# Last sums and residual of one feed-forward taken in token halves, and residual tiles loaded ahead of the norm

## Chip, cores and metric

The kernel runs on one core of a Trainium2 chip. The metric is the device time of one execution in microseconds, lower is better; the time before is the median of three executions.

## The reference, cut to what matters

Two layers over 1024 tokens of width 1024, all in float32. Each sub-layer stands between two RMS norms and adds its normed result to the residual stream `h`:

```python
def rms_norm(x, g, eps=1e-6):
    xf = x.astype(jnp.float32)
    y = xf * lax.rsqrt(jnp.mean(xf * xf, axis=-1, keepdims=True) + eps)
    return (y * g.astype(jnp.float32)).astype(x.dtype)
...
def swiglu(y, wg, wu, wd):
    return (jax.nn.silu(y @ wg) * (y @ wu)) @ wd
...
    for l in range(DEPTH):
        y = rms_norm(h, norm_g[l, 0])
        ...
        h = h + rms_norm(y, norm_g[l, 1])
        y = swiglu(rms_norm(h, norm_g[l, 2]), w_gate[l], w_up[l], w_down[l])
        h = h + rms_norm(y, norm_g[l, 3])
```

What stands at the second "..." is the mixer: gated DeltaNet and top-k sparse attention in layer 0, stick-breaking attention and a gated linear recurrence in layer 1, then an output projection of the two concatenated results.

## The kernel before, in words

**Tiling.** Features lie on the 128 partitions and tokens in the columns. The 1024 tokens are taken in two halves of 512, so an activation of width 1024 is eight tiles of 128x512. Every large product is done in three passes: each operand is split into a rounded high part and a low part (the rest), and high x high, low x high and high x low are summed in PSUM (`passes`, L239). ACT makes the high part and DVE or POOL the low part (`split`, L192 and L196). Weights come in units of 128x1024 (`wload`, L227): two loads of 256 KB into `wraw`, split into `whi` and `wlo`; four buffers of each hold two units.

**Stages.** For each half: `outproj` (L418) sums the output projection from the split mixer results `cat`; `after_out` (L528) norms it and adds the residual; `ffn` (L449) does the SwiGLU in six groups of hidden tiles; `after_ffn` (L533) norms and adds again. `h` lives in DRAM between them. `residual` (L385) is the common body: `inv_rms` (L309) sums the squares over partitions with a matmul on ones (L313) and takes the inverse root on ACT (L315, L316). Then for each of the eight tiles the residual is loaded into a `hld` tile (three buffers, L396), the sum is multiplied by gain and inverse root (L397), the residual is added (L398) and the result stored (L399). Where `late` is set, `y_tile` (L334) at once splits the result, still unnormed, into `yhi` (ACT, L339) and `ylo` (DVE, L343) for the next product, and `norms` sums its squares (L302, L305, L306).

**The last group of an FFN.** The eight sums of the last group are added to `part` (L489), each followed by its square and the squares' add. The very last FFN of the kernel uses `down_halves` (L497) in their place: for the first 256 columns all eight sums, then for the other 256, each half with squares of its own (L509), and `last_residual` (L513) norms and adds half by half (L524, L525). In `down_halves` a weight unit is loaded anew for each half.

**The pool `act`** (L416) holds 16 tiles of 128x512. It is shared: `outproj` keeps its 16 split `cat` tiles there (L428), an FFN the eight split hidden tiles of a group of four (L469).

**What sets the order.** A scheduler puts the instructions in order on each engine, by priorities and the program's order; `first()` (L185) raises a block's priority. `pace` lets pieces of the sparse attention run between weight units in FFN(0, half 0). In `run` (L1288), FFN(0, half 1) is followed by `after_ffn` whose generator is started, and `outproj(1, 0)` is woven in with it (L1342 to L1348).

Of the kernel before, what the change touches and what calls it, by code (L numbers as in the profile page):

```python
# [12 lines left out]
F32 = mybir.dt.float32  # L13
F32R = mybir.dt.float32r
BF = mybir.dt.bfloat16
U32 = mybir.dt.uint32
AF = mybir.ActivationFunctionType
OP = mybir.AluOpType
# [4 lines left out]
P = 128  # L23
S = 1024
D = 1024
HS = 512
NT = 4
KD = 8
# [83 lines left out]
class Trunk:  # L112
# [272 lines left out]
    def residual(self, l, i, src, dst, parts, acc, nxt, box, late=False):  # L385

        nc = self.nc
        with self.first():
            r = self.inv_rms(acc, "rs", "b")
            acc = None  # L390
            y = Y()
            for k in range(KD):
                p = parts[k]
                rows = slice(k * P, (k + 1) * P)
                h = self.t(self.hp, [P, HS], "hld", bufs=3)
                nc.sync.dma_start(h, src[rows])  # L396
                nc.vector.scalar_tensor_tensor(p, p, self.ng(l, i, k), r, op0=OP.mult, op1=OP.mult)  # L397
                nc.vector.tensor_tensor(out=p, in0=p, in1=h, op=OP.add)  # L398
                nc.sync.dma_start(dst[rows], p)  # L399
                if late:  # L400
                    self.y_tile(y, k, p, self.ng(*nxt, k))
                elif nxt is not None:
                    acc = self.sumsq(acc, k, p)
            if late:
                self.norms(y, parts, nxt[1] == 0)
                box.append(y)
        if nxt is not None and not late:
            yield
            with self.first():
                r = self.inv_rms(acc, "rs", "b")  # L410
            yield
            with self.first():
                box.append(self.to_y(*nxt, parts, r))
        yield
# [98 lines left out]
    def last_residual(self, src, dst, parts, halves):  # L513
        nc = self.nc
        with self.first():
            hs = []
            for k in range(KD):
                hs.append(self.t(self.tail, [P, HS], "tail"))
                nc.sync.dma_start(hs[k], src[k * P:(k + 1) * P])
            for i, (c, acc) in enumerate(halves):  # L520
                r = self.inv_rms(acc, ("rs", "rd")[i], "b")
                for k in range(KD):
                    p, h = parts[k][:, c], hs[k][:, c]
                    nc.vector.scalar_tensor_tensor(p, p, self.ng(1, 3, k), r, op0=OP.mult, op1=OP.mult)  # L524
                    nc.vector.tensor_tensor(out=p, in0=p, in1=h, op=OP.add)  # L525
                    nc.sync.dma_start(dst[k * P:(k + 1) * P, c], p)

    def after_out(self, l, half, parts, box, late=False):  # L528
        cols = slice(half * HS, (half + 1) * HS)
        src = self.ins["x"][:, cols] if l == 0 else self.h[1][half]  # L530
        return self.residual(l, 1, src, self.h[2 * l][half], *parts, (l, 2), box, late)
# [756 lines left out]
    def run(self):  # L1288
        tc = self.tc
        every = lambda gen: deque(gen, maxlen=0)  # L1290
# [5 lines left out]
        y = self.first_norm(0)  # L1296
# [3 lines left out]
        y = self.first_norm(1)  # L1300
        with self.since(mark - BOOST0):
            self.deltanet_setup(pool)
            self.dsa_setup(pool)
            b = self.dsa(pool, 0)
# [9 lines left out]
        y1, o, f, y = y, [], [], []  # L1314
# [3 lines left out]
        self.tm_store(U_VB, y1, self.vb[1])  # L1318
        self.slow = slow
        every(self.after_out(0, 0, o, y, True))  # L1320
        every(self.ffn(0, y[0], f))
        every(self.after_ffn(0, 0, f, y, True))
        self.proj_d(0, y[1])
        self.finish()
        m0.close()
# [7 lines left out]
        y0, o, f, y = y[1], [], [], []  # L1333
        every(self.outproj(0, 1, o, "hld"))
        r = self.after_out(0, 1, o, y)
# [6 lines left out]
        r = self.after_ffn(0, 1, f, y, True)  # L1342
        next(r)
        o0, y0 = [], []
        g = self.outproj(1, 0, o0, "stage")
# [3 lines left out]
        r = self.after_out(1, 0, o0, y0)  # L1349
# [8 lines left out]
        f0, o, f, y = [], [], [], []  # L1358
        g = self.ffn(1, y0[0], f0)
# [7 lines left out]
        r = self.after_out(1, 1, o, y)  # L1367
# [105 lines left out]
```

## Time and profile before

| | us |
|---|---|
| median of three executions (2882.89 to 2889.29) | 2888.78 |
| the profiled execution's own time | 2889.96 |
| its span, first to last instruction | 2888.2 |
| PE (TensorE) busy | 2819.6 (98%) |
| DVE (VectorE) busy | 1674.9 (58%) |
| ACT (ScalarE) busy | 1580.7 (55%) |
| POOL (GpSimd) busy | 1117.3 (39%) |
| mean granted TensorE clock | 0.992 |

The span is one execution recorded by the hardware; the time around it is 1.8 us. A busy share is an average over the whole span, so a stage is read from windows and timelines of its own. In a timeline row, what stands in brackets is how long the engine was idle before it and what ended the wait. The granted clock is 1.00 at 2.4 GHz and 0.50 at 1.2 GHz; a mean between them is a stretch with both.

### The profile page before, as it was taken

To read this page: it belongs to the slowest core of one execution; us is meant where nothing else is said; L and a number is where in the kernel's file an instruction comes from. 1 tells how busy PE (TensorE), PEld (TensorE's weight loads), DVE (VectorE), ACT (ScalarE), POOL (GpSimd) and SP (SyncE) were. 2 spreads that over 40 slices of the span, in tenths; PEclk is the share of its full clock that TensorE was granted. 3 is DMA by queue.
4 is the path that set the end of the run, shared out by engine and by line. 5 is a ranking of instruction groups with operands and counts; after the bars stand their busy time and mean duration, and the time that the engine had idled before them with its cause. 6 is when DMAs were issued, how large, how long until landed. Compare 5 with 4: busy or idle time off the path is not lost. (4 is left out here: it accounts for less than half of the span.)

```text
span 2888.2 us, 42444 instructions
## 1 busy us (share of the span) xinstructions
PE 2819.6 (98%) x14850; PEld 2352.7 (81%) x14850; DVE 1674.9 (58%) x3037; ACT 1580.7 (55%) x2893; POOL 1117.3 (39%) x916
## 2 busy tenths in 40 slices
PE   8999999999999998999999999999999999999997
PEld 6888898878887876988888888889778778888886
DVE  8757964674756557377655235836665545822235
ACT  5555854667666575264665334536666554543334
POOL 3424332344435342255554323226555532333322
PEclk9999999999999999999999999999999999999999
DMA  6443456344333334445333333644333223543333
GB/s 208 135 125 105 149 164 196 97 138 120 98 120 102 104 120 137 146 151 184 114 112 99 95 95 121 238 159 129 95 99 103 92 86 118 185 144 95 97 97 106
DMA packets 261748, 366.69 MB, mean 127 GB/s; under 512 B 23296, under 2 KB 111392, under 8 KB 261536
## 3 DMA queue, kind: packets, MB, share of 16 engines
q1 hardware_dynamic: 261536, 364.00, 40.0%
q8 instruction: 117, 1.92, 0.3%
q14 instruction: 95, 0.78, 0.1%
HBM read 306.23 MB, written 57.67 MB: 126 GB/s over the span
## 5 line engine op out<-in xcount | busy, mean ns | idle before, releaser
L196 POOL TENSOR_TENSOR wlo<-wraw,whi 128x512 fp32r<-128x512 f32 x422 | 588.8, 1395 | 1292.0 <-PE acc L252 526.7
L192 ACT ACTIVATE whi<-wraw 128x512 fp32r<-128x512 f32 x844 | 522.3, 625 | 480.5 <-PE acc L252 385.2
L196 DVE TENSOR_TENSOR wlo<-wraw,whi 128x512 fp32r<-128x512 f32 x422 | 346.2, 821 | 426.5 <-PE acc L252 334.7
L252 PE MATMUL acc<-yhi,whi 128*128 128x512 f32 x2064 | 582.6, 398 | 8.1 <-ACT whi L192 5.9
L252 PE MATMUL acc<-ylo,whi 128*128 128x512 f32 x2064 | 583.4, 398 | 1.0 <-DVE ylo L343 0.9
L252 PE MATMUL acc<-yhi,wlo 128*128 128x512 f32 x2064 | 537.5, 396 | 0.0
L252 PE MATMUL acc<-act,whi 128*128 128x512 f32 (+1 forms) x1984 | 508.1, 393 | 7.0 <-DVE part L489 1.8
L252 PEld LDWEIGHTS acc<-yhi,whi 128*128 128x128 f32 x2064 | 385.3, 189 | 92.7 <-ACT whi L192 6.4
L252 PEld LDWEIGHTS acc<-ylo,whi 128*128 128x128 f32 x2064 | 387.1, 189 | 88.0 <-issue 6.2
L252 PEld LDWEIGHTS acc<-yhi,wlo 128*128 128x128 f32 x2064 | 383.7, 188 | 86.2 <-issue 9.0
L252 PEld LDWEIGHTS acc<-act,whi 128*128 128x128 f32 x1984 | 365.3, 190 | 95.1 <-issue 7.9
L252 PE MATMUL acc<-act,wlo 128*128 128x512 f32 (+1 forms) x992 | 267.1, 387 | 0.8 <-POOL wlo L196 0.8
L252 PEld LDWEIGHTS acc<-act,wlo 128*128 128x128 f32 x992 | 182.4, 188 | 38.1 <-POOL wlo L196 1.6
L959 ACT ACTIVATE pen<-sc,tk 128x384 bf16<-128x384 f32 (+4 forms) x155 | 155.3, 1002 | 41.8 <-DVE tk L963 38.2
L489 DVE TENSOR_TENSOR part<-acc,part 128x512 f32<-128x512 f32 x152 | 103.5, 685 | 66.7 <-PE acc L252 66.6
L192 ACT ACTIVATE act<-stage 128x512 fp32r<-128x512 f32 x104 | 65.3, 629 | 132.9 <-DVE stage L468 114.1
L196 POOL TENSOR_TENSOR act<-stage,act 128x512 fp32r<-128x512 f32 x88 | 117.6, 1337 | 33.7 <-ACT act L192 30.7
L461 DVE TENSOR_TENSOR stage<-acc,stage 128x512 f32<-128x512 f32 x66 | 45.5, 690 | 109.4 <-ACT stage L219 107.3
L306 DVE TENSOR_TENSOR ssq<-ssq,sq 128x512 f32<-128x512 f32 (+1 forms) x119 | 97.2, 817 | 18.7 <-ACT sq L305 15.8
L960 DVE TENSOR_SCALAR tk<-tk 128x1 uint32<-128x1 f32 x186 | 39.2, 211 | 110.6 <-ACT pen L959 109.8
L252 PE MATMUL acc<-whi,yhi 128*128 128x256 f32 x640 | 98.8, 287 | 1.4 <-DVE stage L561 1.0
L252 PE MATMUL acc<-whi,ylo 128*128 128x256 f32 x640 | 97.2, 285 | 0.0
(461 smaller groups left out, 4009.7 us busy)
## 6 DMA issues: line engine op xcount, KB each, us to landing
wraw<-in_w_units_dram SPq DMA_DIRECT2D x844, 256.0 KB, 2.7
h<-part SPq DMA_DIRECT2D x40, 256.0 KB, 4.0
hld<-h SPq DMA_DIRECT2D x40, 256.0 KB, 4.8
qkvT<-stage SPq DMA_DIRECT2D x24, 256.0 KB, 2.3
kT<-kbT SPq DMA_DIRECT2D x24, 256.0 KB, 3.9
vv<-vb SPq DMA_DIRECT2D x24, 256.0 KB, 2.9
qkv<-qkvT SPq DMA_DIRECT2D x18, 256.0 KB, 3.1
part<-in_x_dram SPq DMA_DIRECT2D x16, 256.0 KB, 5.1
```

The costliest lines, as they stand in the source:

```text
L192: nc.scalar.activation(hi, src, AF.Copy)
L196: e.tensor_tensor(out=lo[:, c], in0=src[:, c], in1=hi[:, c].bitcast(F32), op=OP.subtract)
L252: mm(ps, l, r, start=first and g not in begun, stop=last and end[g] == i)
L306: nc.vector.tensor_tensor(out=acc, in0=acc, in1=sq, op=OP.add)
L461: nc.vector.tensor_tensor(out=s, in0=pg, in1=s, op=OP.mult)
L489: nc.vector.tensor_tensor(out=parts[d], in0=ps, in1=parts[d], op=OP.add)
L959: sc.activation(pen, s, AF.Sign, scale=sg, bias=nb, accum_out=n)
L960: v.tensor_scalar(rej.bitcast(U32), n, th, float(1 << b), op0=OP.is_lt, op1=OP.mult)
```

## The change

In every `residual`, the eight residual tiles are loaded into tiles of the pool `act` ahead of `inv_rms`, in place of `hld` tiles loaded one by one behind it. FFN(0, half 0) takes its last sums by `down_halves`, and a new `residual_halves` norms, adds and splits first 256 columns of all eight tiles, then the other 256; it stores whole tiles in the second round. Lines behind the first edit move: L397 and L398 become L399 and L400 in `residual`, and in `residual_halves` the product is L545, the add L546, the low part L548.

```diff
--- before.py
+++ after.py
@@ -386,14 +386,16 @@
 
         nc = self.nc
         with self.first():
+            hs = []
+            for k in range(KD):
+                hs.append(self.act())
+                nc.sync.dma_start(hs[k], src[k * P:(k + 1) * P])
             r = self.inv_rms(acc, "rs", "b")
             acc = None
             y = Y()
-            for k in range(KD):
+            for k, h in enumerate(hs):
                 p = parts[k]
                 rows = slice(k * P, (k + 1) * P)
-                h = self.t(self.hp, [P, HS], "hld", bufs=3)
-                nc.sync.dma_start(h, src[rows])
                 nc.vector.scalar_tensor_tensor(p, p, self.ng(l, i, k), r, op0=OP.mult, op1=OP.mult)
                 nc.vector.tensor_tensor(out=p, in0=p, in1=h, op=OP.add)
                 nc.sync.dma_start(dst[rows], p)
@@ -524,6 +526,30 @@
                     nc.vector.scalar_tensor_tensor(p, p, self.ng(1, 3, k), r, op0=OP.mult, op1=OP.mult)
                     nc.vector.tensor_tensor(out=p, in0=p, in1=h, op=OP.add)
                     nc.sync.dma_start(dst[k * P:(k + 1) * P, c], p)
+
+    def residual_halves(self, l, i, src, dst, parts, halves, nxt):
+
+        nc = self.nc
+        with self.first():
+            hs, y = [], Y()
+            for k in range(KD):
+                hs.append(self.act())
+                nc.sync.dma_start(hs[k], src[k * P:(k + 1) * P])
+                y.t.append(tuple(self.t(self.yp, [P, HS], f"{n}{k}", F32R) for n in ("yhi", "ylo")))
+            accs = []
+            for j, (c, acc) in enumerate(halves):
+                r = self.inv_rms(acc, ("rs", "rd")[j], "b")
+                for k, (p, h) in enumerate(zip(parts, hs)):
+                    hi, lo = (t[:, c] for t in y.t[k])
+                    g = self.ng(*nxt, k)
+                    nc.vector.scalar_tensor_tensor(p[:, c], p[:, c], self.ng(l, i, k), r, op0=OP.mult, op1=OP.mult)
+                    nc.vector.tensor_tensor(out=p[:, c], in0=p[:, c], in1=h[:, c], op=OP.add)
+                    nc.scalar.activation(hi, p[:, c], AF.Copy, scale=g)
+                    nc.vector.scalar_tensor_tensor(lo, p[:, c], g, hi.bitcast(F32), op0=OP.mult, op1=OP.subtract)
+                    if j:
+                        nc.sync.dma_start(dst[k * P:(k + 1) * P], p)
+            self.norms(y, parts, nxt[1] == 0)
+            return y
 
     def after_out(self, l, half, parts, box, late=False):
         cols = slice(half * HS, (half + 1) * HS)
@@ -1318,8 +1344,8 @@
         self.tm_store(U_VB, y1, self.vb[1])
         self.slow = slow
         every(self.after_out(0, 0, o, y, True))
-        every(self.ffn(0, y[0], f))
-        every(self.after_ffn(0, 0, f, y, True))
+        every(self.ffn(0, y[0], f, True))
+        y.append(self.residual_halves(0, 3, self.h[0][0], self.h[1][0], f[0], f[1:], (1, 0)))
         self.proj_d(0, y[1])
         self.finish()
         m0.close()
```

Where the order of instructions moves (names: tile and number; a name is a number of the program, which differs between the two kernels).

**DVE, after FFN(0, half 1), where outproj(1, 0) begins.** `act<-stage` is the low part of a `cat` tile, here the last three of eight; L306 adds a square, `wlo` is a weight's low part, L397 the first two of the residual's eight products. Before:

```order
L196 TENSOR_TENSOR act_17652<-stage_17649,act_17651 128x512
L196 TENSOR_TENSOR act_17658<-stage_17655,act_17657 128x512
L306 TENSOR_TENSOR ssq_17349<-ssq_17349,sq_17503 128x512
L196 TENSOR_TENSOR act_17664<-stage_17661,act_17663 128x512
L196 TENSOR_TENSOR wlo_17755<-wraw_17752,whi_17754 128x512
L397 SCALAR_TENSOR_TENSOR part_15100<-part_15100,gg_77,rs_17508 128x512
L397 SCALAR_TENSOR_TENSOR part_15115<-part_15115,gg_77,rs_17508 128x512
```

Now, from the last adds of the residual (L400) on; `act_17866` is the low part of the fifth `cat` tile, `act_17872` of the sixth:

```order
L400 TENSOR_TENSOR part_15419<-part_15419,act_17736 128x512
L400 TENSOR_TENSOR part_15446<-part_15446,act_17738 128x512
L400 TENSOR_TENSOR part_15461<-part_15461,act_17740 128x512
L196 TENSOR_TENSOR act_17866<-stage_17863,act_17865 128x512
L343 SCALAR_TENSOR_TENSOR ylo_3817_17751<-part_15320,gg_77,yhi_3816_17750 128x512
L343 SCALAR_TENSOR_TENSOR ylo_3819_17758<-part_15335,gg_77,yhi_3818_17757 128x512
L306 TENSOR_TENSOR ssq_17803<-ssq_17803,sq_17805 128x512
L196 TENSOR_TENSOR act_17872<-stage_17869,act_17871 128x512
L343 SCALAR_TENSOR_TENSOR ylo_3821_17765<-part_15362,gg_77,yhi_3820_17764 128x512
L343 SCALAR_TENSOR_TENSOR ylo_3823_17772<-part_15377,gg_77,yhi_3822_17771 128x512
```

The low parts of the last four `cat` tiles stood ahead of the eight products; now they stand behind the eight products and the eight adds, and among the `ylo` of the next norm.

**PE at the same place, now.** `act_17865` and `act_17866` are the high and low part of the fifth `cat` tile, `act_17871` and `act_17872` of the sixth, `act_17841` to `act_17859` high parts of the first four; this is 33 rows behind the first matmul of outproj(1, 0):

```order
L252 MATMUL acc_17887<-act_17865,whi_17927 128x512
L252 MATMUL acc_17888<-act_17865,whi_17927 128x512
L252 MATMUL acc_17970<-act_17841,wlo_17975 128x512
L252 MATMUL acc_17970<-act_17847,wlo_17975 128x512
L252 MATMUL acc_17970<-act_17853,wlo_17981 128x512
L252 MATMUL acc_17970<-act_17859,wlo_17981 128x512
L252 MATMUL acc_17887<-act_17871,whi_17927 128x512
L252 MATMUL acc_17888<-act_17871,whi_17927 128x512
L252 MATMUL acc_17887<-act_17866,whi_17927 128x512
L252 MATMUL acc_17888<-act_17866,whi_17927 128x512
L252 MATMUL acc_17887<-act_17872,whi_17927 128x512
L252 MATMUL acc_17888<-act_17872,whi_17927 128x512
```

Outproj's matmuls on the first four `cat` tiles stand ahead of these and between them; the first reading of the eighth tile's low part has 54 of outproj's 192 matmuls ahead of it.

**PE behind the last sums of FFN(0, half 0).** L252 is the last of the sums' matmuls, L313 the norm's matmul, the rest belongs to sparse attention and DeltaNet. Before:

```order
L252 MATMUL acc_11460<-act_11203,wlo_11440 128x512
L252 MATMUL acc_11460<-act_11290,wlo_11440 128x512
L748 MATMUL a_6054<-qkv_1310_6010,qkv_1311_6012 128x128 x4
L1038 MATMUL w_9855<-cc_76,lg_9841 128x128 x4
L1038 MATMUL w_9862<-cc_76,lg_9841 128x128 x4
L1044 MATMUL w_9869<-vv_9835,pt_9860 128x128 x4
L753 MATMUL a_6060<-cc_76,qkv_1311_6012 128x128 x4
L1018 MATMUL w_9890<-kT_9879,qb_9828 128x512
L1044 MATMUL w_9869<-vv_9835,pt_9867 128x128 x4
L1018 MATMUL w_9893<-kT_9879,qb_9828 128x512
L313 MATMUL b_11477<-ssq_11320,cc_76 128x512
```

Now, from the row behind the last sum of the second half on:

```order
L785 MATMUL a_6067<-cc_76,qkv_1312_6014 128x128 x4
L313 MATMUL b_11692<-ssq_11320,cc_76 128x256
L1064 MATMUL w_9855<-cc_76,lg_9841 128x128 x4
L1064 MATMUL w_9862<-cc_76,lg_9841 128x128 x4
L796 MATMUL a_6076<-cc_76,tt_6073 128x128 x4
L1070 MATMUL w_9869<-vv_9835,pt_9860 128x128 x4
L1044 MATMUL w_9890<-kT_9879,qb_9828 128x512
L1070 MATMUL w_9869<-vv_9835,pt_9867 128x128 x4
L1044 MATMUL w_9893<-kT_9879,qb_9828 128x512
L803 MATMUL a_6084<-tn_6081,nt_6045 128x128 x4
L808 MATMUL a_6090<-tt_6073,y_6083 128x128 x4
L313 MATMUL b_11729<-ssq_11503,cc_76 128x256
```

The first half's norm (`ssq_11320`) does not stand among the second half's sums: it is the second row behind all of them, and the second half's norm (`ssq_11503`) is ten rows further.

## Rows read from the trace of the kernel before

**Rows 1.** The page: busy time by engine; DMA issues, with KB and us to landing.
```profile
PE 2819.6 (98%) x14850; PEld 2352.7 (81%) x14850; DVE 1674.9 (58%) x3037; ACT 1580.7 (55%) x2893; POOL 1117.3 (39%) x916
...
wraw<-in_w_units_dram SPq DMA_DIRECT2D x844, 256.0 KB, 2.7
```

**Rows 2.** Windows: length, busy time by engine (instructions), granted clock, DMA share, GB/s.
```profile
1062.70:1091.00 28.30, 26.67 (x121) 20.64 (x119) 26.50 (x48) 15.29 (x28) 13.97 (x12) 1.00 0.25 74
...
1119.00:1126.50 7.50, 6.75 (x23) 5.49 (x23) 6.95 (x14) 5.59 (x10) 0.00 (x0) 0.54 0.89 291
1091.00:1131.00 40.00, 30.74 (x151) 23.33 (x152) 33.36 (x67) 22.02 (x39) 5.99 (x5) 0.83 0.53 166
...
1787.40:1833.80 46.40, 46.40 (x206) 37.55 (x205) 40.05 (x53) 31.93 (x59) 12.22 (x8) 1.00 0.57 193
```

**Rows 3.** Timeline of PE: start, us, instructions, [idle before <- releaser].
```profile
1114.19 0.73 PE L252 MATMUL acc<-yhi,whi 128*128 128x512 f32 x2 [2.05 <-ACT yhi L339]
...
1115.56 2.11 PE L252 MATMUL acc<-yhi,whi 128*128 128x512 f32 x4
```

**Rows 4.** Timeline of DVE in the first residual after an FFN.
```profile
1106.97 5.81 DVE L397 SCALAR_TENSOR_TENSOR part<-part,gg,rs 128x512 f32<-128x512 f32 x8 [0.36 <-ACT rs L316]
1112.70 1.28 DVE L398 TENSOR_TENSOR part<-part,hld 128x512 f32<-128x512 f32 x2
...
1130.03 0.74 DVE L343 SCALAR_TENSOR_TENSOR ylo<-part,gg,yhi 128x512 fp32r<-128x512 f32 x1
```

**Rows 5.** Timelines of PE and DVE: matmuls of 512 columns, then the last FFN.
```profile
1781.93 1.98 PE L252 MATMUL acc<-act,whi 128*128 128x512 f32 x8
1783.74 1.07 PE L252 MATMUL acc<-act,wlo 128*128 128x512 f32 x4
...
2851.49 1.12 PE L252 MATMUL acc<-act,whi 128*128 128x256 f32 x8
2852.45 0.64 PE L252 MATMUL acc<-act,wlo 128*128 128x256 f32 x4
...
2878.21 3.25 DVE L524 SCALAR_TENSOR_TENSOR part<-part,gg,rd 128x256 f32<-128x256 f32 x8 [1.85 <-ACT rd L316]
2881.38 2.76 DVE L525 TENSOR_TENSOR part<-part,tail 128x256 f32<-128x256 f32 x8
```

**Rows 6.** Timelines of ACT, PE and DVE from the sums' end into outproj(1, 0).
```profile
1771.37 1.26 ACT L192 ACTIVATE act<-stage 128x512 fp32r<-128x512 f32 x2 [3.58 <-DMA stage<-cat]
...
1787.37 1.98 PE L252 MATMUL acc<-act,whi 128*128 128x512 f32 x8
...
1795.08 1.02 PE L313 MATMUL b<-ssq,cc 128*128 128x512 f32 x2
...
1794.94 0.69 DVE L196 TENSOR_TENSOR act<-stage,act 128x512 fp32r<-128x512 f32 x1 [2.02 <-ACT act L192]
...
1797.52 6.42 DVE L397 SCALAR_TENSOR_TENSOR part<-part,gg,rs 128x512 f32<-128x512 f32 x8 [0.18 <-ACT rs L316]
```

**Rows 7.** Timelines of DVE and PE at two residuals after outproj, and one window.
```profile
581.54 1.29 DVE L398 TENSOR_TENSOR part<-part,hld 128x512 f32<-128x512 f32 x1 [1.42 <-DMA hld<-in_x_dram]
...
583.48 0.66 PE L788 MATMUL a<-cc,tt 128*128 128x128 f32 x4 [1.34 <-DVE tt L783]
...
1311.90 0.69 DVE L398 TENSOR_TENSOR part<-part,hld 128x512 f32<-128x512 f32 x1 [3.85 <-DMA hld<-in_x_dram]
...
1315.27 0.69 DVE L398 TENSOR_TENSOR part<-part,hld 128x512 f32<-128x512 f32 x1 [1.47 <-DMA hld<-in_x_dram]
...
1324.69 2.05 PE L1246 MATMUL a<-vi,d 128*128 128x128 f32 x8 [2.85 <-DVE sq L844]
...
1323.00:1332.00 9.00, 7.31 (x22) 5.58 (x23) 5.61 (x9) 3.59 (x7) 2.04 (x2) 0.62 0.87 291
```

**Rows 8.** Timeline of POOL: two weight splits.
```profile
1301.99 4.91 POOL L196 TENSOR_TENSOR wlo<-wraw,whi 128x512 fp32r<-128x512 f32 x1 [5.98 <-PE acc L252]
1307.93 1.27 POOL L196 TENSOR_TENSOR wlo<-wraw,whi 128x512 fp32r<-128x512 f32 x1 [1.03 <-issue]
```

## The prediction

> **What bounds the kernel now.** I read the page's engine table first: TensorE (PE) is busy 2819.6 of 2888.2 us [rows 1], so time can only be won where PE stands still, runs at its lower clock, or gets fewer matmul columns. Then I listed PE's idle stretches and looked at who ended each. At the two places that the change rewrites, it is VectorE (DVE) that decides. The windows show it [rows 2]: from 1062.7 to 1091 (last sums of FFN(0, half 0)) PE works 26.67 of 28.30 us and DVE 26.50; from 1091 to 1131 (norm and residual) PE works 30.74 of 40 and DVE 33.36, and PE's mean granted clock there is 0.83. PE's last long wait there is for the first `yhi`, up to 1114.19 [rows 3]. The half clock (1.2 GHz) shows as four 512-column matmuls in 2.11 us, where eight take 1.98 at 2.4 GHz [rows 3, 5]; it follows the stretch in which PE waited. Third, the place after FFN(0, half 1), 1787.4 to 1833.8: PE is busy in all of its 46.40 us [rows 2]. Nothing can be won there, only lost. Last, the residual adds that wait for their `hld` tile [rows 7].
>
> **The sum** starts at the profiled execution's own 2889.96 us, which lies 1.2 above the median of 2888.78.
>
> **A. FFN(0, half 0) in halves, 1062.7 to 1131.** *PE:* 96 matmuls of 512 columns become 192 of 256. Eight of 512 start at 1781.93 and their successor at 1783.74, 1.81 later; eight of 256 at 2851.49 and 2852.45, 0.96 apart [rows 5]. That is 96 x 0.2265 = 21.7 against 192 x 0.120 = 23.0, so +1.3. *DVE:* eight gain products of 512 columns take 5.81 us [rows 4], sixteen of 256 take 2 x 3.25 = 6.5 [rows 5]; sum adds, squares' adds, residual adds and `ylo` go from 8 x 0.64 = 5.1 (two in 1.28 [rows 4]) to 16 x 0.345 = 5.5 each (eight in 2.76 [rows 5]); four more weight units bring four splits of 0.69 (the split's row in [rows 6]). Sum 0.7 + 4 x 0.4 + 2.8 = 5.1 us. POOL gets four splits more and ACT eight; both have room in these windows [rows 2]. A weight unit (two loads) is now used up in 24 x 0.120 = 2.9 us; a load lands in 2.7 [rows 1], and the buffers hold two units, so weights cost nothing as long as a landing stays under about twice that. DVE did 59.9 us of work in the 68.3 us of the two windows; 65 now leaves 3 us of slack. So what the halves are for does not come: the order shows the first half's norm on PE only behind all sums of the second half, and on DVE all sums ahead of its first product. With DVE full, the last add comes some 5 us later; the first projection matmul waits for the second half's gain products, adds and `yhi`, about 1121 instead of 1114, and the last `ylo`, which comes faster at 256 columns, ends at 1129 to 1132 against 1130.8 [rows 4]. PE's idle moves from behind the sums into them. **A = 0**, the ends below.
> Ends of A: if idle and low clock both go, 40 - 30.74 = 9.3 of idle and 40 x (1 - 0.83) = 6.8 of clock, 6.3 of it with PE at work, come back, less 1.3: -14.3. If the DVE work all lands on the path (5.1) and the low clock costs as much again as half of now (3): +8.
>
> **B. Residual tiles in `act` at after_ffn(0, half 1), 1787.4.** The `act` pool has 16 tiles. The last FFN group holds eight; before, the other eight took the first `cat` splits of outproj(1, 0) from 1771.37 on, while sums still ran, and the rest followed by 1794.94 [rows 6]. Now eight residual tiles take them. So `cat` 0 to 3 wait for the FFN's last matmuls and `cat` 4 to 7 for tiles that the residual adds give back. In the order their low parts stand on DVE behind all eight products and all eight adds. Count from the outproj's start, T = 1787.37: today products start at T+10.2 (1797.52), with four `cat` splits ahead of them; I take T+7, since the norm's matmul, which starts at T+7.7 now (1795.08), stands only ten matmuls into outproj in the new order. Eight products 5.9 (mean of 5.81 and 6.42 [rows 4, 6]): T+12.9. Then 23 DVE instructions (eight adds, one weight split, four `cat` splits, eight `ylo`, two squares' adds) at 0.62 = 14.3 up to the low part of `cat` 7: T+27.2. PE has 54 of outproj's 192 matmuls ahead of the one that reads it; 138 x 0.2265 = 31.3 remain, and 0.9 for norm matmuls among them: T+59.4, against T+46.4 now. **+13.0.** Ends: products at T+5 and no POOL contention, +10; products at T+10.2 as today, +16. What is queued behind: the same DVE queue holds the eight `ylo` of the next norm, due only after outproj, so nobody else waits. The low clock: PE works only some 13 of those 27 us, less than in 1091 to 1131; there 1119 to 1126.5 was granted 0.54 with PE busy 6.75 of 7.5 [rows 2], which lost 3.4. I take **+2.5**, between 0 and 5. The Trainium skill, "TensorE: Matmul & The Clock Gate", section "HAM oscillation — how this bites in real kernels", says that a wait between stretches of matmuls sends the next stretch off at half clock; by it this term would be nearer its upper end, 5, and the sum 2901. The rows agree.
>
> **C. Loads ahead at the other residuals.** At 1311.90 and 1315.27 DVE waits 3.85 and 1.47 us for `hld`; behind them stands a reduction whose chain over POOL ends in PE's wait of 2.85 us at 1324.69, after which 1323 to 1332 is granted 0.62 [rows 7]: 7.31 busy at that mean clock loses up to 3.4 more. With the tiles there ahead, DVE reaches the reduction some 5 us sooner. Of 2.85 + 3.4 I take 5. At 581.54 DVE waits 1.42, and PE 1.34 at 583.48 [rows 7]: 1.5 with the smaller wait behind. **C = -6.5**, between 0 (the burst of eight loads lands as late as now, since DMA, not the buffers, was late) and -8. The other three residuals have no PE idle beside them; 0, covered by dense PE work, and up to +3 if the eight loads, which stand ahead of weight loads in SyncE's queue, delay one by a whole landing of 2.7 [rows 1].
>
> Sum: 2889.96 + 0 + 13.0 + 2.5 - 6.5 = **2899.0 us**, 0.35% above the median.
>
> **Rivals.**
> 1. *Stage A pays after all.* The norm's wait hides, PE stays at 2.4 GHz: A = -14.3, 2884.7. For it: idle and low clock stand there plainly [rows 2, 3]. Against: DVE is full, and the order puts both norms behind all sums. Decides: a first projection matmul clearly before 1114. This is the not-slower side.
> 2. *B is covered.* The first four `cat` tiles feed PE for 54 matmuls, 12.2 us. If the low part of `cat` 7 comes by T+18, outproj ends at 18 + 31.3 + 0.9 = T+50.2, and B costs 4, too little to lower the clock: 2889.96 + 4 - 6.5 = 2887.5. Against: DVE would have to do products and 23 instructions in 11 us, or the products would have to start ahead of the sums' end. Decides: that T+18.
> 3. *Stage A gets worse.* DVE's extra 5 us and POOL's splits lie on the path: A = +8, 2907. For it: DVE 26.50 of 28.30 [rows 2]; a POOL split that ran beside DVE's products took 4.91 us, another 1.27 [rows 8]. The Trainium skill, "SBUF — State Buffer", section "SBUF: two separate sides", says that VectorE with two SBUF inputs and GpSimd exclude each other from a shared port for a whole instruction; the rows agree. By it four more POOL splits of about 1.3 would each stop DVE, some 5 us more in A.
> 4. *The change does not do what it says*: in stage A it does not, as far as the norm goes; that is in the forecast.
>
> **Chances.** Forecast 0.52 (time 2892 to 2907), rival 1 0.22, rival 2 0.10, rival 3 0.16. A measurement can tell about 0.3%, 8.7 us, from no change: faster is under 2880.1, slower over 2897.4. Faster needs rival 1 with a B at its low end or with rival 2: 0.09. The forecast's lower part (0.13) and most of rivals 1 and 2 (0.23): same 0.36. The rest of the forecast and rival 3: slower 0.55. Range: 2885 leaves out the lower part of rival 1 (about 0.13), 2911 the upper part of rival 3 (0.06).
>
> **What would show it.** B right: PE idle of 10 us or more between the FFN(0, half 1) sums and the end of outproj(1, 0), released by DVE's `act<-stage`, with a granted clock under 1.00 there; wrong: that stretch still runs 46 to 50 us. A right: PE idle inside the sums, ended by DVE's 256-column adds, and about 9 us of it; wrong: idle gone from both windows. C right: no DVE wait for residual loads, and no PE gap of 2.85 with its low clock. The prediction falls if stage A gives over 8 us, or B costs under 6.

## The result, and the profile after

The changed kernel takes **2907.73 us** (median; 2904.75 to 2908.17) against 2887.34 for the kernel before: +20.4 us. The ratio is 1.0066, 95% interval [1.0048, 1.0084], or +19.1 us [13.9, 24.3]. Of the prediction (2899.0, range 2885 to 2911, slower 0.55) the sign and the range held; the size was half of what came (10.2 us above its median), and the time lies just over the forecast's own band, 2892 to 2907.

| us | before | after |
|---|---|---|
| median | 2887.34 | 2907.73 |
| span of the profiled execution | 2888.2 | 2906.2 |
| PE busy | 2819.6 | 2825.8 |

The page of the changed kernel, its span and busy times (before: [rows 1]):

```profile
span 2906.2 us, 42790 instructions
...
PE 2825.8 (97%) x14948; PEld 2360.0 (81%) x14948; DVE 1686.6 (58%) x3080; ACT 1591.4 (55%) x2919; POOL 1116.1 (38%) x920
```

PE is busy 6 us longer and DVE 12; in the other 12 us of the longer span PE is idle.

**Behind FFN(0, half 1).** Windows of the changed kernel (length, busy by engine, granted clock, DMA share, GB/s): the stage that answers to the last of [rows 2], from the first matmul of outproj(1, 0) to the first on `yhi` (206 matmuls, as there), and two pieces of it.

```profile
1789.93:1851.53 61.60, 52.71 (x206) 39.70 (x204) 38.21 (x54) 34.12 (x61) 10.79 (x8) 0.89 0.45 143
1805.00:1818.00 13.00, 10.20 (x21) 6.27 (x22) 13.00 (x21) 9.94 (x18) 0.00 (x0) 0.50 0.66 222
1818.00:1822.00 4.00, 4.00 (x19) 3.29 (x18) 3.67 (x6) 3.22 (x7) 1.05 (x1) 1.00 0.00 0
```

The stage took 46.40 us with PE always busy; now it takes 61.6 with PE busy for 52.7. So 8.9 of the 15.2 us more are PE's waits, and in 6.3 PE is busy longer with the same 206 matmuls: from 1805 to 1818 all that runs is at half clock, and from 1818 on at full clock. PE's, DVE's and ACT's timelines there (start, us, instructions, idle before and releaser; before: [rows 6]):

```profile
1789.93 1.61 PE L252 MATMUL acc<-act,whi 128*128 128x512 f32 x6
1792.76 1.20 PE L252 MATMUL acc<-act,whi 128*128 128x512 f32 x4 [1.23 <-DVE act L196]
...
1796.12 1.66 PE L252 MATMUL acc<-act,whi 128*128 128x512 f32 x6 [0.38 <-ACT act L192]
...
1805.07 1.22 PE L252 MATMUL acc<-act,whi 128*128 128x512 f32 x2 [4.55 <-ACT act L192]
...
1809.83 1.22 PE L252 MATMUL acc<-act,whi 128*128 128x512 f32 x2 [0.75 <-DVE act L196]
1812.36 1.22 PE L252 MATMUL acc<-act,whi 128*128 128x512 f32 x2 [1.31 <-DVE act L196]
1814.25 4.74 PE L252 MATMUL acc<-act,whi 128*128 128x512 f32 x12 [0.67 <-ACT act L192]
...
1851.53 1.07 PE L252 MATMUL acc<-yhi,whi 128*128 128x512 f32 x4
```

```profile
1797.34 6.41 DVE L399 SCALAR_TENSOR_TENSOR part<-part,gg,rs 128x512 f32<-128x512 f32 x8 [0.55 <-ACT rs L316]
...
1805.48 3.69 DVE L400 TENSOR_TENSOR part<-part,act 128x512 f32<-128x512 f32 x6
...
1816.14 0.74 DVE L343 SCALAR_TENSOR_TENSOR ylo<-part,gg,yhi 128x512 fp32r<-128x512 f32 x1
1816.80 1.28 DVE L196 TENSOR_TENSOR act<-stage,act 128x512 fp32r<-128x512 f32 x2
```

```profile
1788.09 0.63 ACT L192 ACTIVATE act<-stage 128x512 fp32r<-128x512 f32 x1 [1.77 <-PE acc L252]
...
1804.39 0.63 ACT L192 ACTIVATE act<-stage 128x512 fp32r<-128x512 f32 x1 [5.89 <-DVE part L400]
```

PE waits six times for a low or high part of a `cat` tile, 4.55 us at 1805.07. The slots show in ACT's rows: the first `cat` split starts at 1788.09, where it started at 1771.37 [rows 6], and the fifth, which ends PE's longest wait, had itself waited 5.89 us for the residual's adds, which give a slot back. DVE does its eight products (6.41) and the adds first and has no pause from 1805 to 1818; the last two `cat` splits end at 1818.08, 28.2 us into the stage. (ACT's high parts of these two tiles also wait for their loads, 1.05 and 0.42 us, but DVE is at other work meanwhile.) The next product on `yhi` starts at 1851.53; before, at 1833.80.

**FFN(0, half 0).** The two windows that answer to the first and third of [rows 2], moved by the 4.1 us that the execution was late there already:

```profile
1066.80:1095.10 28.30, 23.42 (x174) 20.89 (x173) 26.48 (x48) 16.98 (x35) 17.30 (x13) 1.00 0.54 177
1095.10:1135.10 40.00, 29.83 (x176) 24.99 (x175) 39.65 (x104) 23.13 (x50) 8.26 (x8) 0.87 0.48 163
```

In the sums PE's share falls from 26.67 to 23.42 of 28.30, and behind them from 30.74 to 29.83 of 40, where DVE is now busy for 39.65. So PE is idle 4.9 us inside the sums, where it was 1.6, and 10.2 behind them, where it was 9.3. The clock behind them is 0.87, where it was 0.83. PE's and DVE's timelines (before: [rows 3, 4]):

```profile
1087.47 1.18 PE L252 MATMUL acc<-act,whi 128*128 128x256 f32 x8 [0.97 <-DVE part L511]
...
1097.08 1.19 PE L252 MATMUL acc<-act,whi 128*128 128x256 f32 x8 [1.32 <-DVE part L511]
...
1117.87 1.76 PE L808 MATMUL a<-tt,y 128*128 128x128 f32 x8 [4.51 <-DVE y L804]
...
1130.74 2.19 PE L252 MATMUL acc<-yhi,whi 128*128 128x512 f32 x7
```

```profile
1108.99 3.26 DVE L545 SCALAR_TENSOR_TENSOR part<-part,gg,rs 128x256 f32<-128x256 f32 x8 [0.19 <-ACT rs L316]
...
1121.98 3.24 DVE L545 SCALAR_TENSOR_TENSOR part<-part,gg,rd 128x256 f32<-128x256 f32 x8
```

Inside the sums PE waits for 256-column adds. DVE's products of the first half start at 1108.99, which is 2.1 us sooner than before (1106.97 and 4.1), but those of the second half follow only 13 us later, and the first projection matmul, which needs both, comes at 1130.74, 12.4 us later than before (1114.19 and 4.1). In between PE waits 4.51 us for other work of DVE.

**Where the time went.** For a ledger I took the start of the same weight splits on ACT in each trace (median over the splits of a stretch, the four added units left out) and subtracted the first trace of the kernel before. A row of the table is worked out from the trace of that kernel and the first one; all the kernels but the first are those of the next section. Between columns 1050 and 1210 lies FFN(0, half 0) with its residual, between 1270 and 1365 the residual after outproj(0, 1), between 1600 and 1830 the place behind FFN(0, half 1).

| shift, us, at | 470 | 1050 | 1210 | 1270 | 1365 | 1600 | 1830 | 2700 |
|---|---|---|---|---|---|---|---|---|
| changed kernel | 2.9 | 4.2 | 8.5 | 8.5 | 1.6 | 3.3 | 17.7 | 17.5 |
| before, again (e5) | 2.6 | 3.2 | 0.9 | 0.9 | -5.6 | -5.6 | -6.2 | -7.3 |
| loads ahead only (e1) | 5.3 | 5.0 | 2.8 | 2.8 | -4.1 | -2.3 | 12.1 | 11.2 |
| halves only (e2) | 0.2 | 0.9 | 4.9 | 4.9 | -2.0 | -2.0 | -2.7 | -2.2 |
| all but B (e3) | 4.6 | 5.6 | 7.8 | 7.7 | 0.8 | 2.4 | 1.9 | 1.3 |
| loads ahead, no B, no halves (e4) | 3.2 | 4.3 | 4.5 | 4.5 | -2.3 | -0.6 | -1.3 | -1.6 |
| sums in halves (e6) | 2.3 | 3.5 | 4.7 | 5.0 | 3.8 | 2.0 | 1.2 | 1.0 |
| residual in halves (e7) | 5.4 | 7.1 | 6.3 | 6.1 | -3.7 | -2.6 | -3.2 | -3.0 |
| the same again (e11) | 2.7 | 3.6 | 2.1 | 4.6 | -7.8 | -6.4 | -7.0 | -8.1 |
| B: five tiles, no `act` (e8) | 5.1 | 6.2 | 3.8 | 4.1 | -0.4 | -0.1 | -0.8 | 1.0 |
| B: four tiles in `act` (e10) | 1.8 | 2.4 | 2.2 | 1.7 | -0.7 | -0.6 | 11.4 | 10.3 |

The first column is a warning: up to 500 us the order of the instructions is the same in all of them, and they differ by up to 5 us. The four executions whose order is that of the kernel before up to 1760 us (the first trace, e5, e8, e10) warn once more: from 1050 to 1600 they shift by 0, -8.8, -6.3 and -3.0 us against the first. So a step of a few us in one trace may be chance, and in e7 and e11, where the splits are woven in anew behind stage A, the columns up to 1365 are rough besides. Totals below are from timed runs.

### The profile page after: what moved, and what is told of

It is laid out like the page before. It is cut to its first block, busy times and chain, and to the rows that moved or that the text cites. A ratio compares the mean times of both kernels' runs of the same rounds, so it can differ in the third digit from the quotient of the medians.

```text
span 2906.2 us, 42790 instructions
## 1 busy us (share of the span) xinstructions
PE 2825.8 (97%) x14948; PEld 2360.0 (81%) x14948; DVE 1686.6 (58%) x3080; ACT 1591.4 (55%) x2919; POOL 1116.1 (38%) x920
## 5 line engine op out<-in xcount | busy, mean ns | idle before, releaser
L252 PE MATMUL acc<-yhi,whi 128*128 128x512 f32 x2064 | 581.0, 397 | 6.6 <-ACT whi L192 5.6
L252 PE MATMUL acc<-ylo,whi 128*128 128x512 f32 x2064 | 579.9, 396 | 0.5 <-DVE ylo L343 0.3
L252 PE MATMUL acc<-act,whi 128*128 128x512 f32 (+1 forms) x2048 | 514.4, 388 | 23.2 <-ACT act L192 5.6
L252 PE MATMUL acc<-yhi,wlo 128*128 128x512 f32 x2064 | 535.6, 396 | 0.0
L252 PEld LDWEIGHTS acc<-act,whi 128*128 128x128 f32 x2048 | 370.1, 191 | 113.4 <-ACT act L192 9.7
L252 PEld LDWEIGHTS acc<-yhi,whi 128*128 128x128 f32 x2064 | 384.4, 189 | 90.7 <-issue 6.5
L252 PEld LDWEIGHTS acc<-ylo,whi 128*128 128x128 f32 x2064 | 385.6, 188 | 86.9 <-issue 5.4
L252 PEld LDWEIGHTS acc<-yhi,wlo 128*128 128x128 f32 x2064 | 383.7, 188 | 85.2 <-issue 7.8
L252 PE MATMUL acc<-act,wlo 128*128 128x512 f32 (+1 forms) x1024 | 269.2, 382 | 0.7 <-POOL wlo L196 0.7
L252 PEld LDWEIGHTS acc<-act,wlo 128*128 128x128 f32 x1024 | 185.8, 189 | 37.8 <-issue 1.7
L306 DVE TENSOR_TENSOR ssq<-ssq,sq 128x512 f32<-128x512 f32 (+1 forms) x126 | 104.5, 830 | 21.1 <-ACT sq L305 17.3
L252 PE MATMUL acc<-whi,yhi 128*128 128x256 f32 x640 | 98.9, 287 | 1.0 <-DVE stage L587 0.6
L252 PE MATMUL acc<-whi,ylo 128*128 128x256 f32 x640 | 97.6, 286 | 0.0
```

Source lines behind the costliest of these rows:

```text
L252: mm(ps, l, r, start=first and g not in begun, stop=last and end[g] == i)
L306: nc.vector.tensor_tensor(out=acc, in0=acc, in1=sq, op=OP.add)
```

## The experiments

**Theory 1**, from the ledger: stage A (FFN(0, half 0)) costs 4 us, B (the `act` slots behind FFN(0, half 1)) 14.5, the loads ahead elsewhere give back 10. **Theory 2**: the halves carry most of the loss. **Rival at B**: loading ahead as such, its burst of loads and the order that follows, costs the time, not the shortage of slots.

| | kernel | median, us | before, us | ratio [95%] |
|---|---|---|---|---|
| e1 | loads ahead only | 2901.24 | 2885.48 | 1.0052 [1.0039, 1.0065] |
| e2 | halves only | 2892.29 | 2885.48 | 1.0021 [1.0012, 1.0030] |
| e3 | whole change but B | 2891.14 | 2885.48 | 1.0022 [1.0012, 1.0031] |
| e4 | loads ahead without B | 2887.88 | 2885.48 | 1.0006 [0.9995, 1.0016] |
| e6 | sums in halves | 2897.48 | 2887.20 | 1.0032 [1.0020, 1.0043] |
| e7 | residual in halves | 2883.66 | 2887.20 | 0.9984 [0.9975, 0.9994] |
| e8 | B: five tiles, no `act` | 2889.00 | 2887.20 | 1.0008 [0.9998, 1.0018] |
| e9 | e6, units loaded once | 2892.36 | 2886.72 | 1.0015 [1.0005, 1.0024] |
| e10 | B: four tiles in `act` | 2901.77 | 2886.72 | 1.0051 [1.0036, 1.0066] |
| e11 | e7 again | 2883.21 | 2886.72 | 0.9986 [0.9977, 0.9994] |

### e1 to e4: the parts, alone and left out

For e1, e3 and e4 `residual` is told its half and loads ahead only at listed places; elsewhere it takes `hld` tiles as before. e1 lists all six calls of `residual`, e3 and e4 all but (0, 3, 1); e1 and e4 have the old lines in `run`. e2 lists none and keeps `residual_halves`, which loads its own eight tiles ahead into `act`.

```diff
-            for k in range(KD):
+            for k in range(KD if (l, i, half) in LOAD_AHEAD else 0):
                 hs.append(self.act())
...
-            for k, h in enumerate(hs):
+            for k in range(KD):
...
+                if hs:
+                    h = hs[k]
+                else:
+                    h = self.t(self.hp, [P, HS], "hld", bufs=3)
+                    nc.sync.dma_start(h, src[rows])
```

Expected of e1:

> Only the loads ahead, at all seven residuals that are taken whole; FFN(0, half 0) as before. Theory 1 (the traces' ledger: stage A costs 4.4 us, the act slots behind FFN(0, half 1) cost 14.5, loads ahead at the two residuals after outproj of layer 0 give back 10): 4 us slower than before, 16 faster or so than the changed kernel only through the missing halves' 4 us and side effects on the woven sparse attention, so between +2 and +9. One more act user, after_ffn(0, 0), is in it. Theory 2 (the halves carry most of the loss): no slower than before.

The text counts one residual too many: in e1 the one after FFN(0, half 0) keeps `hld`. Measured: +15.0 (2885.48 x 0.0052). Theory 2 falls; theory 1 had put too much on the gain.

> Only the halves: every whole residual loads its tiles into hld as before. Theory 1: +4 us, up to +8 if the re-weaving of the sparse attention costs something of its own. Theory 2 (the halves carry most of the loss): +12 or more.

Measured: +6.1 [3.5, 8.7]. Theory 1, and theory 2 is out.

> The whole change but for one residual: the one after FFN(0, half 1) keeps its hld tiles. Theory 1: the 14.5 us there go, so about 6 us slower than before, and outproj(1, 0) runs its 46 us without an idle stretch. Rival (the burst of loads ahead, not the slots, delays things): 15 us or more slower still.

Measured: +6.3 [3.5, 8.9]. The window that answers to the stage, in e3:

```profile
1789.80:1836.20 46.40, 46.40 (x205) 37.37 (x204) 39.67 (x52) 31.89 (x59) 12.57 (x9) 1.00 0.60 202
```

PE is busy in all 46.40 us again. B is worth 0.0066 - 0.0022 = 0.44%, **12.7 us**, by leaving it out, and 0.0052 - 0.0006 = 0.46%, **13.3 us**, by e1 against e4, each with some 5 us either way (an estimate from the intervals of the two ratios); its step in the traces, from 1600 to 1830, is 14.4 in both.

> Loads ahead at all residuals but the one after FFN(0, half 1), and no halves. Theory 1: the gain of the two residuals after outproj of layer 0 is left alone, about 10 us faster than before (2877). Rival (bursts of loads ahead cost something everywhere): no faster than before.

Measured: +1.7 [-1.4, +4.6]. This is the miss of theory 1: the 10 us are not there. Where they went is in the table: from 1270 to 1365 e4 makes up 6.8 us, but so do e2 (6.9), which loads nothing ahead there, and e5 (6.5), which is the kernel before.

### e5: the kernel before, once more

No edit.

> The kernel before once more, for its trace. Theory 1 (the idle stretch of 2.85 us at 1324.69 and the low clock behind it come from one weight split on POOL that took 4.91 us at 1301.99 in that one execution, and held up the loads queued behind the weight load that waited for it): that split takes about 1.8 us here, no PE gap there, and the stretch from 1270 to 1365 of the first trace is some 7 us shorter. Rival (the waits for hld cause it whenever this kernel runs): the gap of about 2.85 us is there again.

POOL's timeline at that place in e5, in the changed kernel, and in e8 and e10 (below), which there have the code of the kernel before:

```profile
1302.86 1.83 POOL L196 TENSOR_TENSOR wlo<-wraw,whi 128x512 fp32r<-128x512 f32 x1 [5.98 <-PE acc L252]
```

```profile
1310.50 1.83 POOL L196 TENSOR_TENSOR wlo<-wraw,whi 128x512 fp32r<-128x512 f32 x1 [5.98 <-PE acc L252]
```

```profile
1306.08 4.91 POOL L197 TENSOR_TENSOR wlo<-wraw,whi 128x512 fp32r<-128x512 f32 x1 [5.98 <-PE acc L253]
```

```profile
1303.69 4.90 POOL L197 TENSOR_TENSOR wlo<-wraw,whi 128x512 fp32r<-128x512 f32 x1 [5.98 <-PE acc L253]
```

And PE's timeline behind it in e8:

```profile
1327.28 1.13 PE L1279 MATMUL a<-vi,d 128*128 128x128 f32 x8 [1.35 <-DVE sq L877]
```

The split that took 4.91 us [rows 8] takes 1.83 in e5, and PE has no wait there; the execution took 2883.11 us. But it is not one accident: e8 has 4.91 again and e10 4.90, with PE waits of 1.35 and 2.23 us. Of five traces with this code and order (before, e2, e5, e8, e10) three have the long split. SyncE's queue shows what it holds up (start, us, line, transfer, count), in the kernel before:

```profile
1297.83 0.41 SPq L1056 DMA_DIRECT2D qc<-qcT  x1
1306.93 0.33 SPq L233 DMA_DIRECT2D wraw<-in_w_units_dram  x1
...
1307.79 0.42 SPq L396 DMA_DIRECT2D hld<-in_x_dram  x1
...
1309.33 1.23 SPq L396 DMA_DIRECT2D hld<-in_x_dram  x2
```

The same weight load and the later of DVE's two waits for `hld` (before: [rows 7]) in e5:

```profile
1304.71 0.33 SPq L233 DMA_DIRECT2D wraw<-in_w_units_dram  x1
```

```profile
1313.14 0.69 DVE L398 TENSOR_TENSOR part<-part,hld 128x512 f32<-128x512 f32 x1 [0.81 <-DMA hld<-in_x_dram]
```

In the first trace nothing is issued for 9 us: the weight load at 1306.93 needs the buffer of the split that ended at 1306.90, and the `hld` loads queue up behind it. In e5 the split ends at 1304.69 and the load goes out at 1304.71; DVE then waits 0.15 and 0.81 us for `hld`, where it waited 3.85 and 1.47. The residual's loads were late because POOL was, and PE's wait follows from that. The long split does not explain all of it: e8 and e10 have it too and make up 4.5 and 2.4 us from 1270 to 1365. So theory 1 holds for e5 (it took 6.5 us less from 1270 to 1365), and the rival's "whenever this kernel runs" is wrong, but so is "that one execution". In the four traces with loads ahead at this residual (changed, e1, e3, e4) the split takes 1.82 or 1.83; whether the loads ahead cause that, or chance, four traces don't settle. What they do show is a price: from 1365 to 1600 these four lose 1.6 to 1.8 us each, e2 and e5 none; what takes it was not looked for.

### e6, e7, e9, e11: stage A taken apart

e6 keeps `down_halves` for FFN(0, half 0), and takes the residual whole, with `hld` tiles: the inverse roots of the two halves are put side by side in one tile.

```diff
+            if isinstance(acc, list):
+                r = self.t(self.hp, [P, HS], "rs", bufs=1)
+                for c, a in acc:
+                    ps = self.mx("b")[:, c]
+                    nc.tensor.matmul(ps, self.ones, a, start=True, stop=True)
...
-        y.append(self.residual_halves(0, 3, self.h[0][0], self.h[1][0], f[0], f[1:], (1, 0)))
+        every(self.after_ffn(0, 0, (f[0], f[1:]), y, True))
```

> FFN(0, half 0) takes its last sums in halves, and the residual behind it is taken whole, as before, with both halves' inverse roots side by side; no loads ahead. Theory 1 (the sums in halves are the price: four more weight units and their splits on a full DVE, 1.3 us of PE): +4 to +6, most of what the halves cost together. Rival (the residual in halves is the price: the next projection needs both halves anyway): 0 to +2.

Measured: +9.2 [5.8, 12.4]. e7 is the other half: sums whole, `residual_halves` behind them.

```diff
-        every(self.ffn(0, y[0], f, True))
-        y.append(self.residual_halves(0, 3, self.h[0][0], self.h[1][0], f[0], f[1:], (1, 0)))
+        every(self.ffn(0, y[0], f))
+        y.append(self.residual_halves(0, 3, self.h[0][0], self.h[1][0], f[0], [(c, f[1][:, c]) for c in (slice(0, HS // 2), slice(HS // 2, HS))], (1, 0)))
```

> The last sums whole as before, the residual behind them in halves; no other loads ahead. Theory 1 (the sums in halves are the price): 0 to +2. Rival (the residual in halves is): +4 to +6.

Measured: -4.6 [-7.2, -1.7]. The sums are the price, more than was expected, and the residual in halves gains, which neither expected; since it also loads its tiles ahead into `act`, no run tells which of the two gains. The two results add up to e2's 6 within their intervals. e11 is e7 a second time:

> The last sums whole, the residual behind them in halves, a second time: the version that came out faster than before. If that holds, 2 to 6 us faster; if it was chance, within 1 us of before.

Measured: -4.0 [-6.6, -1.7]. It holds: **this version is faster than both kernels**. But not for the reason one would look for. In stage A itself e11 shows this (PE's timeline):

```profile
1120.92 3.81 PE L253 MATMUL acc<-yhi,whi 128*128 128x512 f32 x8 [5.83 <-ACT yhi L553]
```

PE waits 5.83 us in one piece for `yhi`, where the kernel before has 2.05 [rows 3]. Stage A's step in the table is -0.8 (e7) and -1.5 (e11), in e5 -2.3: no gain. A gain shows later, among the matmuls on `x` of the gated recurrence: the window of 1340 to 1360 in e5, the same in e11, and PE's waits near there in e6:

```profile
1340.00:1360.00 20.00, 17.98 (x192) 17.25 (x191) 13.69 (x19) 9.06 (x17) 17.25 (x18) 1.00 0.38 122
```

```profile
1340.00:1360.00 20.00, 20.00 (x209) 19.49 (x208) 13.98 (x21) 9.25 (x17) 15.39 (x15) 1.00 0.45 148
```

```profile
1341.86 1.16 PE L1251 MATMUL a<-x 128*128 128x128 f32 x8 [2.13 <-POOL x L1246]
...
1348.27 0.73 PE L253 MATMUL acc<-whi,yhi 128*128 128x256 f32 x4 [1.85 <-DVE stage L260]
...
1352.26 0.45 PE L1262 MATMUL a<-x 128*32 128x32 f32 x16 [1.58 <-POOL x L1246]
```

e5 leaves PE idle for 2.0 of the 20 us, e11 for none; e6 waits 2.13, 1.85 and 1.58 us, twice for POOL's `x`. From 1050 to 1600 e7 makes up 9.7 us, e11 10.0, e5 8.8, e2 2.9, e6 1.5. So a part of what an edit in stage A earns or costs may fall due 250 us later, where the scheduler has woven everything anew. That is read from single traces, and a rival stands: e5, the kernel before without the wait behind the long split [rows 7], took 2883.11 us in its one run, as much as e7 and e11 in the median, and neither of these has that wait. Their gain may be no more than that. The totals are sure; where the gain arises, and by what, is not shown.

e9 asks which part of the halved sums costs. Each unit is loaded once, and both halves of its two sums are taken before the next.

```diff
-        for c in (slice(0, HS // 2), slice(HS // 2, HS)):
-            acc = None
+        cols = slice(0, HS // 2), slice(HS // 2, HS)
+        accs = [None, None]
+        for js in (((0, 1),) if once else ((0,), (1,))):
             for d, p in enumerate(parts):
                 if d % nd == 0:
                     w = self.wload(du + d // nd)
-                ps = self.acc()[:, c]
...
+                for h in js:
+                    c = cols[h]
...
```

> As the kernel with the sums in halves and the residual whole, but each weight unit is loaded once and used for both halves of its two sums before the next: the 256-column sums, adds and squares stay, the four additional weight units with their eight loads and sixteen splits go. Theory 1 (the reloaded units and their splits on a full DVE are most of the 9 us): 0 to +4. Rival (256-column matmuls, adds and squares' adds are the price): +6 to +9.

Measured: +4.3 [1.4, 6.9]. It lies between the two expectations: about half of the 9 us goes with the reloaded units, about half stays with the 256-column sums. The intervals of e6 and e9 overlap a little, and e9 also changes the order of the sums, so the halves are rough.

### e8 and e10: is it the slots?

Both change the residual after FFN(0, half 1) alone. e8 loads five of its eight tiles ahead of the norm, three into `hld` and two into a small pool of their own; e10 loads four ahead into `act`.

```diff
-            for k in range(KD if (l, i, half) in LOAD_AHEAD else 0):
-                hs.append(self.act())
+            for k in range(5 if (l, i, half) in LOAD_AHEAD else 0):
+                own = k < 2
+                hs.append(self.t(self.hb if own else self.hp, [P, HS], "hb" if own else "hld", bufs=2 if own else 3))
...
-                if hs:
+                if k < len(hs):
```

> Only the residual after FFN(0, half 1): five of its eight tiles are loaded ahead of the norm, but into three hld tiles and two tiles of a pool of their own, none from act; the other three as before. Theory 1 (the loss there is the shortage of act slots for the cat splits): no slower than before, outproj(1, 0) runs its 46 us with no idle stretch. Rival (loading ahead as such, its burst in the queue and the order that follows): some 5 to 10 us slower.

Measured: +2.3 [-0.6, +5.2], and the stage in e8:

```profile
1786.50:1832.90 46.40, 46.40 (x206) 37.66 (x205) 39.96 (x53) 31.52 (x58) 12.66 (x8) 1.00 0.54 180
```

No idle PE in 46.40 us: loading five tiles ahead costs nothing at B when it takes no slot. All eight tiles were not tried this way.

> Only the residual after FFN(0, half 1), with four of its eight tiles loaded ahead into act, the other four into hld as before. In its order the low parts of six cat tiles stand ahead of the residual's products, and two behind. Theory 1 (shortage of act slots): a part of the loss, 5 to 9 us, with PE waiting for the seventh and eighth cat tile. Rival (a loss of loading ahead as such, or all or nothing): 0 or the full 13.

Measured: +14.7 [10.4, 19.1]; nearly all of the loss is there with four tiles. The stage at B in e10, then PE's timeline and DVE's:

```profile
1786.05:1845.35 59.30, 50.84 (x206) 39.16 (x205) 40.43 (x56) 34.82 (x62) 12.25 (x8) 0.91 0.44 149
```

```profile
1804.23 1.22 PE L253 MATMUL acc<-act,whi 128*128 128x512 f32 x2 [4.50 <-ACT act L193]
1807.53 2.08 PE L253 MATMUL acc<-act,whi 128*128 128x512 f32 x4 [2.08 <-ACT act L193]
1810.36 1.22 PE L253 MATMUL acc<-act,whi 128*128 128x512 f32 x2 [0.75 <-DVE act L197]
1811.38 3.23 PE L253 MATMUL acc<-act,wlo 128*128 128x512 f32 x8
1814.44 2.91 PE L253 MATMUL acc<-act,whi 128*128 128x512 f32 x12
```

```profile
1796.91 5.39 DVE L405 SCALAR_TENSOR_TENSOR part<-part,gg,rs 128x512 f32<-128x512 f32 x8 [1.07 <-ACT rs L317]
...
1807.10 0.68 DVE L197 TENSOR_TENSOR act<-stage,act 128x512 fp32r<-128x512 f32 x1
...
1809.63 0.68 DVE L197 TENSOR_TENSOR act<-stage,act 128x512 fp32r<-128x512 f32 x1
```

Six `cat` tiles are split in time, and PE still waits 4.50 and 2.08 us for the last two: they are split behind the eight products and seven of the adds, at 1807.10 and 1809.63. So theory 1's mechanism stands (the slots), and its "part of the loss" falls. The stage takes 59.3 us with four tiles, 61.6 with eight and 46.4 before; the last `cat` split ends 24.3 and 28.2 us into it. In these two kernels the loss goes by where the *last* `cat` split stands in DVE's queue, and little by how many are late.

## Why the prediction was right or wrong

- **B, +13.0 and +2.5: right in the mechanism and the sum, with the clock's part mis-sized.** Counted from outproj's first matmul (1789.93), the products start at T+7.4 (T+7 was taken) and the low part of `cat` 7 is there at T+28.2 (T+27.2). 0.2 of that is a slip: the mean of 5.81 and 6.42 is 6.1, not 5.9. Outproj ends at T+61.6, where 61.9 was forecast, 59.4 and 2.5 for the clock; that is 15.2 us more than before for a forecast 15.5, and leaving B out gives 12.7 back. But the 2.5 were not the clock. It was at 0.50 while DVE's queue held PE up, and at 1.00 from 1818 on; when the last `cat` split came, at 1818.08, PE had begun just the 54 matmuls that stand ahead of its first reading. So hardly any of the 6.3 us by which PE was busy longer lay on the path. In place of the clock, DVE's queue took 1.0 us more than counted, and the work behind the split 33.4 us for 32.2: that the sum came within 0.3 us is luck. PE's idle time was 8.9 us, under the 10 of the sign, and ACT's `act` ended it as well as DVE's.
- **A = 0: wrong.** The step that failed is "PE's idle moves from behind the sums into them", at no cost: it came inside the sums (4.9 us for 1.6; 9 was the sign) and stayed behind them (10.2 for 9.3). The parts of that step held: PE waits in the sums for DVE's 256-column adds, DVE is full (39.65 of 40), and both norms stand behind all sums. But with DVE full, added DVE work landed on the path: 5.1 us of it were forecast, and the step of stage A is 4.3 in the changed kernel and 4.0 in e2, where e5 has -2.3; timed, e2 is +6.1 [3.5, 8.7]. Which of the added instructions it is, no run separates beyond e9's halves. I had left 3 us of slack in a sum over 68.3 us, as if any DVE instruction could fill any hole; that DVE's holes are waits of its own is how I read the rows, and no run tests it. The first projection matmul came at 1126.6 (1130.74 less the 4.1), where 1121 was forecast. +6 was within the bounds given (-14.3 to +8), near the end that rival 3 named.
- **C = -6.5: wrong.** The step that failed is "at 1311.90 and 1315.27 DVE waits ... for `hld`; ... with the tiles there ahead, DVE reaches the reduction some 5 us sooner". The wait was there, but its cause stood in another group: the split of 4.91 us on POOL [rows 8], which I had used as an example of contention in rival 3 only. It ended at 1306.90, and the late `hld` loads follow from it [rows 7]. The kernel runs with that split at 1.8 us too, and then there is little to gain; what the loads ahead would give with a long split, no trace shows. The sign for C, no PE gap of 2.85 us, came in the changed kernel, but it comes in e2 and e5 as well, which load nothing ahead there. The other 1.5 us, at 583.48, show no gain either: from 470 to 1050 the changed kernel and e4 fall back by 1.3 and 1.1 us, and e5 by 0.6. Timed, the loads ahead without B are +1.7 [-1.4, +4.6].
- **The sum.** 13.0 + 2.5 + 0 - 6.5 = 9 was forecast against the profiled execution, which lay 2.6 us above the median of the result's runs before. Measured by parts: B 12.7 to 13.3, A 6.1, C 0.2 (e3 less e2) to 1.7 (e4), together 19 to 21; the whole is 19.1 by the ratio and 20.4 by the medians. The mechanism that decides was right; two terms were mis-sized, both too kindly.
- **Rivals.** 1 (A pays) is out: e2 is slower. 2 (B is covered) is out: e1 against e4, and the split came at T+28, not T+18; that a B of 4 us is "too little to lower the clock" no run shows. 3 (A gets worse, to 2907): A did, by 6 where it gave 8, together with the forecast's B. That its 2907 is nearly the measured time is luck, since it holds the -6.5 of C, which did not come.

## What to carry to other kernels

When a tile moves to an earlier load, ask whose buffers it takes and where the last holder of such a buffer now stands in the queues: half the borrowed slots cost nearly as much as all, since the last late one decides. A wait seen in one profile needs its cause followed back through the other engines, and a second profile of the same kernel, before a gain is put on it. Work added on the engine that is full inside a stage can land on the path even if the sum over the stage leaves slack, as it did here, and where a scheduler weaves the order, a part of an edit's effect may appear far behind it.

## What the runs showed of the hardware

- One instruction of one program takes 1.8 or 4.9 us. The POOL split beside DVE's eight back-to-back products took 4.91, 4.91 and 4.90 us in three traces and 1.82 and 1.83 in two of the same code. DVE's timeline there in the kernel before, where the split took 4.91, and in e5, where it took 1.83:

```profile
1297.96 5.38 DVE L397 SCALAR_TENSOR_TENSOR part<-part,gg,rs 128x512 f32<-128x512 f32 x8
```

```profile
1298.82 6.41 DVE L397 SCALAR_TENSOR_TENSOR part<-part,gg,rs 128x512 f32<-128x512 f32 x8
```

  The eight products took 5.38 and 6.41 us: where the split was short they were 1.03 us longer, as if it had got in between them. The Trainium skill, "SBUF — State Buffer", section "SBUF: two separate sides", says that the engine which comes second is held off for the whole instruction of the first. The rows agree, and show what that sentence leaves open: POOL was held off over several DVE instructions in a row (4.91 us, where the next split took 1.27 [rows 8] and one product 0.67), so the wait is not bounded by one instruction.
- Executions of the same instructions differ by up to 5 us after 500 us of run, before any edit (first column of the table). A step of 2 us in one trace of this kernel is no evidence.
- Behind FFN(0, half 1) the clock stood at 1.2 GHz from 1805 to 1818, behind a wait of 4.55 us and while PE worked 10.20 of 13 us between shorter ones; from 1818 on, with PE at work without a break since 1814.25, it was at 2.4 GHz. What the low clock costs depends on what the path waits for: in the changed kernel the last `cat` split came as the clock rose, and hardly anything was lost. In e10 the last split was there at 1810.31, and the eight matmuls from 1811.38 still took 3.06 us, where eight take 1.81 at 2.4 GHz [rows 5]: there the first matmuls behind a wait paid for it once more.
